# Two token tiles at once in the query and key norms of both attentions of a two-layer trunk

## The chip, the cores and the metric

The kernel runs on one core of a Trainium2 chip. The metric is the time of one execution on the device in microseconds (us); lower is better. Five engines work side by side, each through its own list of instructions in order: TensorE (PE, matrix products and transposes), VectorE (DVE), ScalarE (ACT), GpSimd (POOL) and SyncE (SP, which issues the DMAs here). They wait for one another through semaphores.

## The reference, cut to what matters

```python
def rmsnorm(x, g):
    y = x * rsqrt(mean(x * x, axis=-1) + 1e-6)
    return y * g

def attn_inputs(h, w_qkv, g_q, g_k, n_kv):
    y = h @ w_qkv                                   # 1024 -> q | k | v
    q = rmsnorm(per_head(y[..., :D_MODEL]), g_q)    # heads of 64
    k = rmsnorm(per_head(y[..., D_MODEL:...]), g_k)
    ...

for i in range(2):                                  # 1024 latent tokens, 256 context tokens
    h = modulate(rmsnorm(x, g_attn[i]), sh1, sc1)
    q, k, v = attn_inputs(h, ...)
    if i == 0: o = neighbourhood_attention(q, k, v, k_c, v_c, rpb)     # 16 heads
    else:                                           # 16 query heads, 4 key/value heads
        q, k = apply_rope(q, cos, sin), apply_rope(k, cos, sin)
        o = sliding_window_attention(q, k, v, k_c, v_c, sink)
    x = x + gt1 * (o @ w_out)
    x = x + gt2 * conv_ffn(modulate(rmsnorm(x, g_ffn[i]), sh2, sc2), ...)
```

## The kernel before

Tokens are cut into tiles of 128: eight latent ones (0 to 7) and two of context (8, 9). All is fp32; large products are made of three passes (high by high, low by high, high by low halves), which is why every weight and activation has a `hi` and a `lo` part.

The first attention goes through eight pairs of heads, and for each through the ten tiles in the order 8, 9, 0 to 7 (`plan_na_qkv`). Per tile: 24 products into a PSUM bank (`mm`), one ACT copy of all 384 columns (q, k, v) to SBUF (`qraw`), then the norm of four heads of 64 (`plan_rstd`): ACT squares (`qsq`), DVE sums per head (`qv`), DVE scales and adds epsilon (one instruction on 128x4), POOL raises to the power -0.5 (`qy`), DVE makes a Newton step (three instructions on 128x4, with `qt`), and DVE multiplies (`qn`). Two tiles' `qn` lie side by side, so that transposes, splits and later steps are already done by pairs of tiles. Around it, `plan_na_su` makes scores (`s`), bias, exponentials, scaling (`S`), transposes (`pt`) and the product with v (`pv`).

The second attention goes through four groups of heads (four query heads and one key head each), per group through tiles 0 to 7 (`plan_sw_qkv`), here tile by tile to the end: five heads normed, then the rotary products `qa` (by the cosine, on DVE or POOL, two instructions) and `qb` (by the sine, on POOL, four instructions), their sum on POOL (two instructions), three transposes on PE. `plan_sw_su` makes scores and the rest. Its softmax has a sink column, which POOL copies (`S<-small`).

The order of the work isn't that of the text. Each attention is planned by a list scheduler (`Sched`, L61): every operation gives its engine or engines, a cost, a key, what it reads and writes, and which buffers of a ring it takes and gives back; the planner walks through its own estimate of time, starts on each engine the operation with the lowest key that is ready and finds its buffers, and the order so found is then written out for every engine. A changed cost or a changed ring moves instructions on all five engines. At the end of each attention the output projection (`o0`, `o1`, `o2` parts) is planned in with the last scores. Weight halves of the next slab (`wlo<-slab`) are made on DVE or POOL.

Of the kernel before, what the change touches and what calls it, by code (L numbers as in the profile page):

```python
# [17 lines left out]
P = 128  # L18
# [205 lines left out]
def trunk_kernel(ctx, tc, xtok, xseq, cc, crow, wmod, wmodt, bmod, gnorm, na_wqkv, na_gqk, na_bias, na_wo,  # L224
# [111 lines left out]
    WG0, WG1 = 4, 5  # L336
    CONV_STEP = 1024
# [115 lines left out]
    def plan_qkv_mm(sc, key, psa, h, tt, slabs, s, J, c0=0, hkey=None):  # L453
# [3 lines left out]
        for kt in range(KT):  # L457
            def mm(e, kt=kt):
# [3 lines left out]
                for i, (a, w) in enumerate(((hh, wh), (hl, wh), (hh, wl))):  # L462
# [5 lines left out]
                  acq=[("mm", J["id"] + ("acc",), 1)] if kt == 0 else (), rel=[("w", i)] if kt % 2 else ())  # L468

    def plan_rstd(sc, key, J, c0, nh, wk, nsq):  # L470

        I = J["id"]

        def sq(e):
            J["sq"] = wk.tile([P, nsq], F32, tag="qsq", name="qsq", bufs=PTB["qsq"])
            act.activation(J["sq"][:, :nh * DH], J["raw"][:, c0:c0 + nh * DH], AF.Square)
        sc.op("act", t_act(nh * DH), sq, reads=[I + ("raw",)], writes=[I + ("sq",)], key=key, acq=[("qsq", I + ("sq",), 1)])

        def red(e):
            v = J["ms"] = tiny.tile([P, 5], F32, tag="qv", name="qv", bufs=4)  # L480
            dve.tensor_reduce(out=v[:, :nh], in_=J["sq"][:, :nh * DH].rearrange("p (h d) -> p h d", d=DH), axis=AX.X,
                              op=ALU.add)
        sc.op("dve", t_dve(nh * DH), red, reads=[I + ("sq",)], writes=[I + ("ms",)], key=key, rel=[I + ("sq",)])

        def mean(e):
            v = J["ms"][:, :nh]
            dve.tensor_scalar(out=v, in0=v, scalar1=1.0 / DH, scalar2=EPS, op0=ALU.mult, op1=ALU.add)
        sc.op("dve", t_dve(0), mean, reads=[I + ("ms",)], writes=[I + ("ms",)], key=key)

        def pw(e):  # L490
            J["y"] = tiny.tile([P, 5], F32, tag="qy", name="qy", bufs=4)
            J["t"] = tiny.tile([P, 5], F32, tag="qt", name="qt", bufs=4)
            pool.tensor_tensor(out=J["y"][:, :nh], in0=J["ms"][:, :nh], in1=mhalf[:, :nh], op=ALU.pow)
        sc.op("pool", 0.42 + nh * 0.165, pw, reads=[I + ("ms",)], writes=[I + ("y",)], key=key)
        ny = lambda: (J["y"][:, :nh], J["t"][:, :nh], J["ms"][:, :nh])

# [10 lines left out]
        for i in range(3):  # L507
            sc.op("dve", t_dve(0), newton(i), reads=[I + ("ms",)], writes=[I + ("y",)], key=key)

# [2156 lines left out]
```

## Time and profile before

| | us |
|---|---|
| three timed runs | 2758.87, 2759.04, 2761.37 (median 2759.04) |
| span of the profiled execution | 2755.5 |
| around the span (median less span; the profiled execution has no time of its own beside the three) | 3.5 |
| PE busy in the span | 2701.9 (98%) |
| DVE busy | 2247.1 (82%) |
| ACT busy | 1684.9 (61%) |
| POOL busy | 340.2 (12%) |

The span has four long stretches: the first attention (about 70 to 650 us), the first feed-forward block with the output projection ahead of it (to about 1610), the second attention (to about 2010) and the second feed-forward block. A table by stretch gives for each engine the busy time and the number of instructions, and the mean TensorE clock that was granted (1.00 is 2.4 GHz, 0.50 is 1.2 GHz). Groups of instructions are rows by operation and shape with busy time, mean duration of one in ns, and the idle time ahead of them with what ended it.

### The profile page before, as it was taken

What the parts mean: (1) busy time and instruction counts of PE and PEld (TensorE: products, weight loads), DVE (VectorE), ACT (ScalarE), POOL (GpSimd) and SP (SyncE); (2) the same over time, 40 slices, a digit from 0 to 9 for tenths busy, and PEclk for the clock granted to TensorE, in tenths of its full rate; (3) what the DMA queues carried; (4) which work ended last, traced back from release to release, by engine and by line L of the source; (5) the groups of instructions that cost most, each with busy time, mean ns of one, the idle gap of its engine ahead of it and who ended that gap; (6) DMA issues with size and microseconds to landing.
All of it is one profiled execution on the core that took longest, in us unless ns stands there. A gap on an engine that the chain in (4) does not pass through costs nothing.

```text
span 2755.5 us, 42708 instructions
## 1 busy us (share of the span) xinstructions
PE 2701.9 (98%) x15300; PEld 2282.4 (83%) x15300; DVE 2247.1 (82%) x4938; ACT 1684.9 (61%) x3000; POOL 340.2 (12%) x520
## 2 busy tenths in 40 slices
PE   7999999998999999999999999999999999999999
PEld 5999999987799988887888877777778788888887
DVE  5988888887778688787887889898877988888757
ACT  6777777776456555555564556666754666656443
POOL 1211111112000000000001007455410000000000
PEclk9999999999999999999999999999999999999999
DMA  7343343335656643334376562143243232334655
GB/s 263 98 127 117 117 135 119 111 96 165 216 170 184 184 142 104 129 118 135 119 249 198 188 201 68 43 129 102 78 152 113 88 115 100 112 107 146 234 175 186
DMA packets 147884, 387.89 MB, mean 141 GB/s; under 512 B 21332, under 2 KB 32084, under 8 KB 147288
## 3 DMA queue, kind: packets, MB, share of 16 engines
q1 hardware_dynamic: 147672, 385.17, 43.2%
q8 instruction: 120, 1.97, 0.3%
q14 instruction: 92, 0.75, 0.1%
HBM read 318.12 MB, written 66.99 MB: 140 GB/s over the span
## 4 chain that ended last, share of the span: by engine, by line
PE 76%; DVE 7%; DMA 2%; issue 2%; POOL 1%; ACT 1%; SPq 0%; DVEq 0%; ACTq 0%; POOLq 0%
PE ua L51 17%; PE uc L51 13%; PE dn L51 12%; PE mm L51 11%; PE pt L51 6%; PE oacc L51 4%; PE ud L51 4%; PE s L51 4%; PE dnc L51 2%; PE pv L51 2%; DVE S L51 1%; DVE wlo L51 1%; DMA woraw<-in_na_wo_dram 1%; DVE xn L51 1%; PE ug L51 0%
## 5 line engine op out<-in xcount | busy, mean ns | idle before, releaser
L51 ACT ACTIVATE whi<-wraw 128x512 fp32r<-128x512 f32 (+1 forms) x264 | 212.3, 804 | 153.6 <-PE uc L51 57.8
L51 DVE TENSOR_TENSOR wlo<-wraw,whi 128x512 fp32r<-128x512 f32 (+1 forms) x264 | 240.6, 912 | 47.7 <-ACT whi L51 47.3
L51 ACT ACTIVATE S<-S,m 128x640 f32<-128x640 f32 (+3 forms) x288 | 220.8, 768 | 63.2 <-DVE m L51 44.9
L51 PE MATMUL dn<-ghi,whi 128*128 128x512 f32 x616 | 240.0, 390 | 0.1
L51 PE MATMUL dn<-glo,whi 128*128 128x512 f32 x616 | 239.9, 389 | 0.2 <-DVE glo L51 0.2
L51 PE MATMUL dn<-ghi,wlo 128*128 128x512 f32 x616 | 239.8, 389 | 0.0
L51 ACT ACTIVATE whi<-s 128x1024 fp32r<-128x1024 f32 (+1 forms) x118 | 110.9, 941 | 182.1 <-PE uc L51 107.7
L51 POOL TENSOR_TENSOR qy<-qv,mhalf 128x4 f32<-128x4 f32 (+1 forms) x114 | 135.3, 1188 | 597.3 <-DVE qv L51 572.1
L51 PE MATMUL pt<-idr,S 128*128 128x128 f32 x1288 | 193.8, 277 | 11.9 <-DVE S L51 4.2
L51 PEld LDWEIGHTS pt<-idr,S 128*128 128x128 f32 x1288 | 151.5, 141 | 45.8 <-issue 12.0
L51 ACT ACTIVATE ghi<-graw 128x512 fp32r<-128x512 f32 x154 | 95.7, 628 | 144.5 <-PE dn L51 85.9
L51 PE MATMUL mm<-whi,h0hi 128*128 128x384 f32 x512 | 180.1, 352 | 0.0
L51 ACT ACTIVATE pt<-pt 128x512 f32<-128x512 f32 (+2 forms) x259 | 133.4, 535 | 64.6 <-PE pt L51 62.7
L51 PE MATMUL mm<-wlo,h0hi 128*128 128x384 f32 x512 | 172.1, 336 | 0.0
L51 DVE TENSOR_TENSOR glo<-graw,ghi 128x512 fp32r<-128x512 f32 x154 | 105.6, 695 | 78.1 <-ACT ghi L51 48.4
L51 DVE TENSOR_TENSOR wlo<-s,whi 128x1024 fp32r<-128x1024 f32 (+1 forms) x118 | 126.9, 1077 | 21.2 <-ACT whi L51 20.8
L51 PEld LDWEIGHTS dn<-ghi,whi 128*128 128x128 f32 x616 | 115.7, 188 | 24.6 <-issue 0.5
L51 PEld LDWEIGHTS dn<-glo,whi 128*128 128x128 f32 x616 | 115.7, 188 | 24.2 <-DVE glo L51 0.5
L51 PE MATMUL ua<-t12hi,whi 128*128 128x512 f32 x344 | 134.8, 392 | 0.9 <-ACT c L51 0.9
L51 PEld LDWEIGHTS dn<-ghi,wlo 128*128 128x128 f32 x616 | 115.6, 188 | 24.0
L51 PE MATMUL ua<-t12lo,whi 128*128 128x512 f32 x344 | 134.0, 390 | 0.0
L51 PE MATMUL ua<-t12hi,wlo 128*128 128x512 f32 x344 | 133.9, 389 | 0.0
(372 smaller groups left out, 8305.2 us busy)
## 6 DMA issues: line engine op xcount, KB each, us to landing
wraw<-in_w_up_dram SPq DMA_DIRECT2D x133, 512.0 KB, 3.8
wmt<-in_wmodt_dram SPq DMA_DIRECT2D x96, 512.0 KB, 4.0
wraw<-in_w_down_dram SPq DMA_DIRECT2D x44, 512.0 KB, 3.7
graw<-g_dram SPq DMA_DIRECT2D x44, 512.0 KB, 4.8
wraw<-in_w_down_dram SPq DMA_DIRECT2D x88, 256.0 KB, 3.0
graw<-g_dram SPq DMA_DIRECT2D x66, 256.0 KB, 2.8
wm<-in_wmod_dram SPq DMA_DIRECT2D x32, 512.0 KB, 6.7
slab<-in_na_wqkv_dram SPq DMA_DIRECT2D x32, 384.0 KB, 3.2
```

The costliest lines, as they stand in the source:

```text
L51: r = f(*a, **k)
```

## The change

Where the planner has seen the first tile of a pair it now only evacuates it; the norm is made for both tiles at the second one. In both attentions:

- the evacuation copies q and k alone (256 or 320 columns) into one half of a buffer of two tiles; v is copied from PSUM by an instruction of its own, and the PSUM bank is given back when both are done;
- one square, one sum per head, one power, one Newton step and one product with the norm for both tiles (8 heads in the first attention, 10 in the second);
- the division by 64 sits in the square's scale, and epsilon is added on POOL ahead of the power; the DVE instruction for both is gone. The Newton step has the same three instructions in another order of factors.

In the second attention also: the normed values go back into the buffer they came from, the squares lie in the buffer of the rotary product (`qa`, two buffers), and `qa`, `qb` and their sum are made for two tiles per instruction (the same number of instructions for two tiles as before for one). `qb` has one buffer. The context tiles of the second attention stay single, with the shorter norm. Counts of the instructions that the change touches (all others are as many, a few of them on another engine):

| | before | after |
|---|---|---|
| norm on DVE, first attention | 6 x 80 tiles | 5 x 40 pairs |
| norm on DVE, second attention | 6 x 32 tiles | 5 x 16 pairs |
| powers on POOL | 80, 32 | 40, 16 (each with an added 128x8 or 128x10 instruction) |
| `qa` on DVE / on POOL | 17 / 15 tiles | 13 / 3 pairs |
| `qb` and sum on POOL | 6 x 32 | 6 x 16 |
| PE | 14174 | 14174 |

```diff
-            act.activation(J["sq"][:, :nh * DH], J["raw"][:, c0:c0 + nh * DH], AF.Square)
+            act.activation(J["sq"][:, :n], src(), AF.Square, scale=DH ** -0.5)
...
-        def mean(e):
-            v = J["ms"][:, :nh]
-            dve.tensor_scalar(out=v, in0=v, scalar1=1.0 / DH, scalar2=EPS, op0=ALU.mult, op1=ALU.add)
-        sc.op("dve", t_dve(0), mean, reads=[I + ("ms",)], writes=[I + ("ms",)], key=key)
...
+            pool.tensor_scalar(out=v, in0=v, scalar1=EPS, scalar2=None, op0=ALU.add)
+            pool.tensor_tensor(out=J["y"][:, :nh], in0=v, in1=mhalf[:, :nh], op=ALU.pow)
+        sc.op("pool", 0.55 + nh * 0.165, pw, reads=[], writes=[I + ("ms",), I + ("y",)], key=key)
...
-    SBUFS, PTB = 5, dict(pt5=6, pt2=4, qsq=2)
+    SBUFS, PTB = 5, dict(pt5=6, pt2=4, qsq=1)
...
-    QA = (("dve", "pool"), (0.85, 1.1))
-    QB = ("pool", 1.55)
+    QA = (("dve", "pool"), (1.25, 1.9))
+    QB = ("pool", 2.1)
...
     def plan_na_qkv(n):
...
-            act.activation(J["raw"], J["acc"][:, :384], AF.Copy)
+            act.activation(f["raw", pr][:, tt % 2, :], J["acc"][:, :256], AF.Copy)
...
-            copy(e, f["v"][tt], pair(J["raw"][:, 256:384]))
+            copy(e, f["v"][tt], pair(J["acc"][:, 256:384]))
...
         if tt % 2 == 0:
             return
+        both = [two + ("raw", 0), two + ("raw", 1)]
+        plan_rstd(sc, key, J, 8, wk, 512, lambda: f["raw", pr].rearrange("p a b -> p (a b)"), both)
...
-    sc = Sched(dict(CAPS, pt5=6, pt2=3, qsq=1, q=10, S=SBUFS, s=4, qraw=3, qa=3, qn=3), near=3.0)
+    sc = Sched(dict(CAPS, pt5=6, pt2=3, qsq=1, q=10, S=SBUFS, s=4, qraw=3, qa=2, qb=1), near=3.0)
...
+            act.activation(B["raw"][:, tt % 2].rearrange("p h d -> p (h d)"), J["acc"][:, :320], AF.Copy)
...
+        plan_rstd(sc, key, B, 10, wk, 640, lambda: B["raw"].rearrange("p t h d -> p (t h d)"), both,
+                  (a_tile, [("qa", two + ("a",), 2)]))
...
+            r = B["raw"].rearrange("p t h d -> p (t h) d")
+            ENG[e].tensor_tensor(out=r, in0=r, in1=B["y"].unsqueeze(2).to_broadcast([P, 10, DH]), op=ALU.mult)
...
+                ENG[e].tensor_tensor(out=B["a"][:, :, s], in0=B["raw"][:, :, s], in1=tab(rc, k, m, slice(0, DH)), op=ALU.mult)
...
+            ENG[e].tensor_tensor(out=a[:, :, 5:6], in0=a[:, :, 4:5], in1=b[:, :, 4:5], op=ALU.add)
+            ENG[e].tensor_tensor(out=a[:, :, :5], in0=a[:, :, :5], in1=b, op=ALU.add)
+        sc.op("pool", t_pool(640) + t_pool(128), qs, reads=[K("b")], writes=[K("a")], key=key, rel=[K("b")])
+        for t in (tt - 1, tt):
+            plan_sw_tr(g, t, key, B, K)
```

Where it stands, at three places.

VectorE where the first attention's last products have ended and its last scores wait for buffers. Before (`S,m` and `m` are the evacuation of scores with its running minimum, named ISA where it adds the bias; the numbers are those of the scores' tiles):

```order
L51 TENSOR_REDUCE qv<-qsq 128x4
L51 CAST kll<-kll 64x256
L51 TENSOR_SCALAR qv<-qv 128x4
L51 TENSOR_SCALAR S,m_8462<-s 128x256
L51 COPY pt_8475<-pt 128x512
L51 COPY pt_8480<-pt 128x128
L51 ISA S,m_8462<-s,bias,m_8462 128x256
L51 ISA m_8462 128x1
L51 TENSOR_TENSOR qt<-qy 128x4
L51 TENSOR_SCALAR S,m_8495<-s 128x256
L51 SCALAR_TENSOR_TENSOR qt<-qt,qv 128x4
L51 ISA S,m_8495<-s,bias,m_8495 128x384
```

After:

```order
L51 TENSOR_TENSOR wlo<-woraw,whi 128x1024
L51 COPY v<-mm 128x128
L51 TENSOR_SCALAR S,m_8017<-s 128x256
L51 TENSOR_SCALAR S,m_8020<-s 128x256
L51 ISA S,m_8017<-s,bias,m_8017 128x384
L51 ISA m_8017 128x1
L51 ISA S,m_8020<-s,bias,m_8020 128x384
L51 ISA m_8020 128x1
L51 TENSOR_SCALAR S,m_8054<-s 128x256
L51 TENSOR_REDUCE qv<-qsq 128x8
```

The Newton step that stood between two evacuations stands behind them now; a weight half and a copy of v stand ahead.

GpSimd inside the second attention, from one power to the next. Before:

```order
L51 TENSOR_TENSOR qy<-qv,mhalf 128x5
L51 COPY S<-small 128x1
L51 TENSOR_TENSOR qa<-qn,rc 128x256
L51 TENSOR_TENSOR qa<-qn,rc 128x64
L51 COPY S<-small 128x1
L51 TENSOR_TENSOR qb<-qn,rs 128x4x32 x2
L51 TENSOR_TENSOR qb<-qn,rs 128x32 x2
L51 TENSOR_TENSOR qa<-qa,qb 128x64
L51 TENSOR_TENSOR qa<-qa,qb 128x320
```

After:

```order
L51 TENSOR_SCALAR qv<-qv 128x10
L51 TENSOR_TENSOR qy<-qv,mhalf 128x10
L51 COPY S<-small 128x1 x4
L51 TENSOR_TENSOR qb<-qraw,rs 128x2x4x32 x2
L51 TENSOR_TENSOR qb<-qraw,rs 128x2x32 x2
L51 TENSOR_TENSOR qa<-qa,qb 128x2x64
L51 TENSOR_TENSOR qa<-qa,qb 128x2x320
```

One such row of work serves two tiles, in wider instructions; most `qa` products have gone to VectorE.

TensorE at the last transposes of the second attention, among the output projection (`mm<-o0`). Before:

```order
L51 MATMUL pt<-idr,S 128x128 x10
L51 MATMUL s<-kkc_17655,q 128x256 x2
L51 MATMUL s<-kkl_17654,q 128x384 x2
L51 MATMUL pt<-idr,qa 128x128 x3
L51 MATMUL mm<-o0hi_22604,whi 128x512
```

After:

```order
L51 MATMUL pt<-idr,S 128x128 x2
L51 MATMUL mm<-o0hi_21664,whi 128x512
L51 MATMUL mm<-o0lo_21666,whi 128x512
L51 MATMUL mm<-o0hi_21664,wlo 128x512
L51 MATMUL pt<-idr,qa 128x128 x6
```

The transposes of two tiles stand together, with products of the projection ahead of them.

## Rows read from the trace of the kernel before

**Rows 1.** Busy time by stretch: bounds, length, each engine's busy us (instructions), clock, DMA

```profile
core 0: us, PE busy (x) PEld busy (x) DVE busy (x) ACT busy (x) POOL busy (x), PEclk, DMA share, GB/s
70.00:620.00 550.00, 546.68 (x3746) 502.65 (x3744) 479.11 (x1694) 408.35 (x964) 86.50 (x77) 1.00 0.37 115
620.00:650.00 30.00, 24.07 (x167) 19.78 (x166) 27.15 (x86) 23.84 (x52) 11.05 (x8) 0.89 0.49 153
...
1640.00:1980.00 340.00, 335.87 (x2296) 262.48 (x2296) 307.95 (x1021) 230.61 (x514) 187.61 (x362) 1.00 0.25 77
1980.00:2010.00 30.00, 26.40 (x175) 17.95 (x172) 28.12 (x85) 23.81 (x51) 13.88 (x30) 1.00 0.40 139
```

**Rows 2.** TensorE's waits from 620 to 650: who, for whom, total, times, longest

```profile
PE pt L51 <- DVE S L51: 1.5, 1, 1.5
PE s L51 <- DVE S L51: 1.4, 1, 1.4
```

**Rows 3.** Busy time by stretch, the seven microseconds behind those waits

```profile
623.00:630.00 7.00, 5.50 (x23) 4.38 (x25) 5.98 (x26) 5.72 (x12) 1.01 (x1) 0.53 0.75 235
```

**Rows 4.** GpSimd in order of time, 619 to 623: start, duration, what

```profile
619.45 2.36 POOL L51 TENSOR_TENSOR wlo<-woraw,whi 128x1024 fp32r<-128x1024 f32 x1
```

**Rows 5.** VectorE in order of time, the same stretch

```profile
619.98 1.86 DVE L51 TENSOR_TENSOR qt<-qy 128x4 f32<-128x4 f32 x1
```

**Rows 6.** TensorE's waits from 1640 to 1980

```profile
PE pt L51 <- DVE S L51: 2.0, 3, 1.3
PE pt L51 <- POOL qa L51: 1.0, 1, 1.0
```

**Rows 7.** GpSimd in order of time, 1786 to 1794

```profile
1789.74 3.74 POOL L51 TENSOR_TENSOR wlo<-slab,whi 128x768 fp32r<-128x768 f32 x2
```

**Rows 8.** VectorE in order of time, the same stretch

```profile
1791.66 2.17 DVE L51 TENSOR_SCALAR S<-S,sm 128x640 f32<-128x640 f32 x1
```

**Rows 9.** Groups by shape, 70 to 630: count, busy us, mean ns, idle before

```profile
L51 POOL TENSOR_TENSOR qy<-qv,mhalf 128x4 f32<-128x4 f32 x76 | 85.2, 1121 | 472.6 <-DVE qv L51 447.9 <-DVE sm L51 23.3 <-DVE qy L51 1.4
...
L51 DVE TENSOR_TENSOR qn<-qraw,qy 128x256 f32<-128x256 f32 x76 | 31.9, 420 | 0.3
...
L51 DVE TENSOR_REDUCE qv<-qsq 128x4 f32<-128x256 f32 x76 | 31.1, 410 | 1.7 <-ACT qsq L51 1.2
...
L51 DVE TENSOR_SCALAR qv<-qv 128x4 f32<-128x4 f32 x76 | 12.2, 161 | 0.2
```

**Rows 10.** Newton steps alone (VectorE instructions on `qt`), both attentions

```profile
70.00:630.00 560.00, 37.54 (x228) 0.99 0.37 116
1615.00:2015.00 400.00, 23.10 (x102) 1.00 0.30 96
```

**Rows 11.** Groups by shape, 1615 to 2015

```profile
L51 POOL TENSOR_TENSOR qy<-qv,mhalf 128x5 f32<-128x5 f32 x32 | 43.6, 1366 | 60.9 <-DVE qv L51 60.3
...
L51 POOL TENSOR_TENSOR qb<-qn,rs 128x128 f32<-128x128 f32 x64 | 31.7, 515 | 30.2 <-DVE qn L51 15.6 <-DVE sm L51 13.4 <-issue 1.2
L51 POOL TENSOR_TENSOR qa<-qa,qb 128x320 f32<-128x320 f32 x32 | 29.9, 935 | 2.5
L51 POOL COPY S<-small 128x1 f32<-128x1 f32 x122 | 29.9, 269 | 1.6 <-ACT S L51 1.6
...
L51 POOL TENSOR_TENSOR qb<-qn,rs 128x32 f32<-128x32 f32 x64 | 17.8, 298 | 0.0
L51 DVE TENSOR_TENSOR qn<-qraw,qy 128x320 f32<-128x320 f32 x32 | 16.1, 503 | 0.2
...
L51 DVE TENSOR_REDUCE qv<-qsq 128x5 f32<-128x320 f32 x32 | 15.3, 478 | 1.1 <-ACT qsq L51 1.0
...
L51 POOL TENSOR_TENSOR qa<-qa,qb 128x64 f32<-128x64 f32 x32 | 10.5, 329 | 0.5
...
L51 DVE TENSOR_SCALAR qv<-qv 128x5 f32<-128x5 f32 x32 | 8.2, 258 | 0.1
...
L51 DVE TENSOR_TENSOR wlo<-woraw,whi 128x1024 fp32r<-128x1024 f32 x4 | 4.9, 1219 | 0.4 <-ACT whi L51 0.4
```

## What was predicted

> **What bounds the kernel now.** I read the busy table first: TensorE is busy in 2701.9 of 2755.5 us (98%), and VectorE, whose work the change cuts, in 82%. The change leaves TensorE's 14174 instructions alone, so the time can fall only by what TensorE waits, or loses to a lower clock, in the two stretches that the change touches. The table by stretch gives that [rows 1]: length less PE's busy time is 3.3 us in the body of the first attention (550 - 546.68), 5.9 in its tail from 620 to 650, 4.1 in the body of the second (340 - 335.87) and 3.6 in its tail from 1980 to 2010. That is 16.9 us. One more loss hides in busy time: in the seven microseconds from 623 the granted clock is 0.53, about the lower of the two levels (1.2 GHz), right after TensorE stood still [rows 3]; 5.50 us of matmuls ran there, of which about 5.50 x (1 - 0.53) = 2.6 us would be gone at the full clock. So **19.5 us, 0.7%, is all that this change can reach**, whatever it saves elsewhere.
>
> Then I asked who ends those waits. From 620 to 650 the two largest, 1.5 and 1.4 us, are transposes and scores waiting for VectorE's evacuation of `S` [rows 2]. GpSimd makes a weight half at 619.45 (2.36 us) [rows 4], and the first Newton instruction, started beside it at 619.98, takes 1.86 us [rows 5], against a mean of 37.54 / 228 = 0.165 us [rows 10]: the tiny instruction ends only when GpSimd is done, and the evacuations queue behind it. In the second attention's body the listed waits are on VectorE's `S` (2.0 us in three) and on GpSimd's `qa` (1.0 in one) [rows 6], and the same sight stands at 1790: a weight half on GpSimd [rows 7], beside it the scaling of `S`, ahead of the transposes, takes 2.17 us [rows 8].
>
> **The change part by part.**
>
> *Norm, first attention.* Per pair before, on VectorE: two sums at 410 ns, two means at 161, six Newton instructions at 165, two products at 420 [rows 9, 10]: 820 + 322 + 990 + 840 = 2972 ns. After: the sum over twice the columns. How much of 410 is per column the trace tells by the second attention's 478 at 64 columns more [rows 11]: 68 per 64, so 410 + 4 x 68 = 682. The product likewise: 503 - 420 = 83 per 64, so 420 + 4 x 83 = 752. Three Newton instructions, 495; no mean. Sum 1929 ns, **1.05 us less per pair, 42 us over 40 pairs**. VectorE falls from 87% to about 79% of the body. It is not what bounds there, so nearly all of it is off the path: the body has 3.3 us of waits in 550. I give it -1.0, with 0 and -3.3 as ends.
>
> *Norm, second attention.* Per pair before 2 x (478 + 258 + 503) [rows 11] + 6 x 226 (23.10 / 102) [rows 10] = 3834 ns. After: 478 + 5 x 68 = 818, 503 + 5 x 83 = 918, 3 x 226 = 678: 2414. **1.4 us less per pair, 23 us over 16**, from 307.95 of 340 busy (91%) to about 85%. `qa` moves towards VectorE, from 17 tiles to 13 pairs: nine tiles more of 320 columns at 83 / 64 = 1.3 ns a column, 3.7 us, less eight instructions' fixed part of about 90 ns (420 - 4 x 83), 0.7: 3 us back.
>
> *GpSimd, second attention.* The power takes 1121 ns at 4 columns and 1366 at 5 [rows 9, 11], so 1366 + 5 x 245 = 2591 at 10, against 2 x 1366 = 2732; the added epsilon is bounded by the nearest small instruction there, 269 ns (`S<-small`). No gain. `qb`: 2 x 515 + 2 x 298 = 1626 per tile, 3252 a pair; with twice the columns 3 x 32 columns cost 217, so 128 columns more 289: 804, and 32 more 72: 370; 2 x 804 + 2 x 370 = 2348. The sum: 935 + 329 = 1264 per tile, 2528 a pair; its columns at (935 - 329) / 256 = 2.37 ns give 1692 + 480 = 2172. So 0.9 + 0.4 = **1.3 us less per pair on GpSimd**. It is 55% busy there (187.61 of 340): what counts of it is the chain, not the share.
>
> *The chain to TensorE, second attention.* From a tile's sum of squares to its transposes before: 478 + 258 + 678 + 1366 + 503 + 1626 + 1264 = 6.2 us. After, for two tiles: 818 + 269 + 678 + 2591 + 918 + 2348 + 2172 = **9.8 us**, 3.6 longer, and the first tile of a pair waits for its partner as well. What covers it is TensorE's work between a pair's last product and its transposes. In the written order the tightest place has 51 TensorE instructions after (49 before), the next ones 54, 73, 76 and 76; 335.87 / 2296 = 0.146 us each by busy time, somewhat more for products of 320 columns. So the cover is about 7.5 to 9 us at the two tightest pairs and 11 or more at the rest, against 9.8 us and the copy and the square ahead of it. I expect up to 2 us of new waiting at the tightest pairs, none at the others, and put **+1.0** (ends 0 and +4).
>
> *The tails.* At 620 the Newton step no longer stands between the score evacuations: they come first now, behind a weight half and a copy of v. The 1.86 us instruction [rows 5] isn't in that row any more, but that half, which GpSimd made in 2.36 us [rows 4], now stands on VectorE, at 1.22 us as four others do [rows 11]. The 2.9 us of waits [rows 2] and the 2.6 us of clock behind them hang together, since the clock fell after the standstill. I take **-4.0** of these 5.5; ends -5.5 and +1, where the half on VectorE delays the evacuations as much as the Newton step did. The second body: VectorE's lighter load and fewer small instructions that meet a GpSimd weight half (four per tile, now three per pair) take half of its 4.1: **-2.0** (ends -4.1, 0). Its tail has 3.6, where TensorE also waits for the last output parts that the change leaves alone: **-1.0** (ends -3, +1).
>
> *The rest.* The square on ScalarE covers two tiles in one instruction; the evacuation is 128 or 64 columns narrower, and the copy of v reads PSUM itself. ScalarE is 61% busy, so I put nothing there; uncovered, v's copy holding the product bank longer (0.4 us a tile at most, by the 410 ns of a 256-column sum [rows 9]) would cost that where the banks run out, which the waits of before don't list. The context tiles are too few to count.
>
> Sum: -1.0 - 4.0 - 2.0 - 1.0 + 1.0 = -7.0. The profiled span of 2755.5 becomes 2748.5; with the 3.5 us around it **2752.0**. Its own range, from the ends that can come together, is 2746 to 2757.
>
> A rule of the Trainium skill speaks against the change. What the rows show first: a VectorE instruction that touches SBUF alone, started beside a wide GpSimd one, lasts until that ends [rows 4, 5, 7, 8]. The skill ("SBUF — State Buffer", section "Who interferes with whom") says that VectorE and GpSimd share ports under a lock held for a whole instruction; it takes a two-input VectorE instruction or a fast mode to contend. By that, each wider GpSimd instruction holds VectorE longer. The trace agrees: the Newton product has two such inputs, the scaling can use a fast mode. By that rule alone the time would be that of the fourth case below.
>
> **The rivals.**
>
> *Nothing moves* (2759). The waits that VectorE's load seems to cause are only where the order was tight; the new order has as many, elsewhere. For it: PE waits only 3.3 us in 550 at a VectorE share of 87%, so less load need not mean less waiting. Against it: the named culprit at 620 is an instruction that the order moves. Price: none of the four gains, and the +1.0 unseen among them; give or take 3.
>
> *All of it goes* (2741). The waits and the lost clock go whole, 19.5 us, less some 1.5 us of the second tail's 3.6 that stay with the output parts: 2759 - 18. For it: VectorE gets 62 us of air. Against: in the tails the last scores follow one another through VectorE (27.15 of 30 us busy, and 28.12) [rows 1] whatever becomes of the norms.
>
> *Pairs come late* (slower, 2767). The longer chain isn't covered: each of the second attention's 16 pairs keeps TensorE waiting for its six transposes by 1 us (the wait on `qa` of before, 1.0 us in one place [rows 6], at every pair), +16, and the gains of 8 above stay. It decides where the cover is shorter than the chain: 9.8 us plus copy, square and queueing, from some 67 instructions of 0.146 us on. For it: one buffer of `qb`, two of `qa`, so pairs hardly overlap; GpSimd also makes weight halves of 3.74 us [rows 7] in between. Against it: only two places are below 67, the next is at 73.
>
> *The lock* (2758). A VectorE instruction caught by GpSimd's power is held for up to 2.6 us instead of 1.4, by its product `qb` and sum for 0.3 to 0.8 us more, and the evacuations behind it with it. If each of the three waits on `S` [rows 6] grows by the 1.2 us of the power, the second body loses 3 x 1.2 = 3.7 where I have -2.0, and the sum is -1.3. It decides where more than two such meetings reach TensorE. Against it: VectorE has half as many small instructions to be caught.
>
> **How the numbers follow.** Forecast 0.48; nothing moves 0.16; all goes 0.14; pairs late 0.16; the lock 0.06. A difference under 0.2% (5.5 us) is about what a measurement can't tell from none, so faster means under 2753.5, slower over 2764.6. Of the forecast's own range 2746 to 2757 I count 0.34 as faster and 0.14 as same. Faster: 0.34 + 0.14 = 0.48. Same: 0.14 + 0.16 + 0.06 = 0.36. Slower: 0.16. The range runs from 2739 (the large gain with 2 us to spare) to 2767 (the late pairs' middle): it leaves out half of that case and a little of the large gain, some 0.12.
>
> **What would show it.** Right: VectorE's busy time falls by about 60 us; from 620 to 650 PE busy comes to 26 or more of 30 at a clock near 1.00; the waits in the second attention stay below 4 us. Wrong: waits of transposes on `qa` in most of the 16 pairs (the pairs come late), or evacuations of `S` that last as long as a GpSimd instruction beside them (the lock), or TensorE's waits at their 17 us though VectorE has its air (nothing moves). A clock below 1.00 anywhere new would break the sum as well: it prices the clock at one place only.

## The result and the profile after

The changed kernel takes **2767.02 us** (median of 7 runs, 2763.11 to 2768.02) against 2758.87 before: a ratio of 1.0029, 95% interval 1.0019 to 1.0038. It is 8 us slower. The forecast was 2752.0, range 2739.0 to 2767.0; the median lies just outside, on the slow side.

The profiled execution has a span of 2766.0 us, 10.5 more than before. (Every execution here that has both a time and a span shows about 1.8 us around the span. So the profiled execution before took about 2757.3 us, less than the median, and 1.7 of the 3.5 us that the table of before puts around the span are scatter; the spans lie further apart than the medians by that.) Three matmuls that both kernels have mark its parts: the first product of the statistics after the first attention (`mp`), the one ahead of the second attention (`pt<-invd,sums`), and `mp` after the second attention. TensorE in order of time (start, duration, what, idle time before and its releaser); first the kernel before:

```profile
701.34 0.60 PE L51 MATMUL mp<-invd,nsum 128*128 128x1 f32 x4 [3.04 <-DVE nsum L51]
...
1627.94 1.05 PE L51 MATMUL pt<-invd,sums 128*128 128x1 f32 x8 [1.84 <-DVE sums L51]
...
2074.65 0.95 PE L51 MATMUL mp<-invd,nsum 128*128 128x1 f32 x8
```

and the changed kernel:

```profile
703.99 0.61 PE L51 MATMUL mp<-invd,nsum 128*128 128x1 f32 x4 [2.41 <-DVE nsum L51]
...
1629.77 1.08 PE L51 MATMUL pt<-invd,sums 128*128 128x1 f32 x8 [1.86 <-DVE sums L51]
...
2086.00 0.94 PE L51 MATMUL mp<-invd,nsum 128*128 128x1 f32 x8
```

So the first attention takes 2.7 us more (703.99 against 701.34) and the second 9.5 (456.2 against 446.7); the feed-forward parts differ by under 1 us each. The table by stretch of the changed kernel (columns as in [rows 1]), with the second attention's body also cut at 1740:

```profile
70.00:620.00 550.00, 544.94 (x3733) 500.28 (x3732) 463.46 (x1416) 394.06 (x939) 75.66 (x74) 1.00 0.38 115
620.00:650.00 30.00, 25.26 (x166) 20.98 (x164) 27.13 (x79) 23.35 (x51) 5.96 (x4) 0.89 0.36 113
...
1640.00:1740.00 100.00, 94.15 (x597) 78.11 (x599) 85.64 (x226) 58.20 (x128) 53.84 (x76) 0.97 0.25 77
1740.00:1980.00 240.00, 239.05 (x1663) 182.76 (x1660) 213.38 (x665) 163.18 (x368) 109.67 (x174) 1.00 0.25 79
...
1980.00:2010.00 30.00, 23.60 (x154) 16.95 (x153) 27.73 (x69) 21.04 (x44) 15.08 (x20) 0.94 0.39 132
```

The same cut before:

```profile
1640.00:1740.00 100.00, 99.42 (x658) 79.57 (x657) 94.49 (x298) 65.55 (x145) 63.38 (x117) 1.00 0.22 67
1740.00:1980.00 240.00, 236.45 (x1641) 182.91 (x1641) 213.46 (x724) 165.06 (x371) 124.23 (x246) 1.00 0.27 82
```

The middle of the second attention gained: TensorE idles for 0.95 us there in place of 3.55. Its first hundred microseconds lost: 5.85 in place of 0.58, at a granted clock of 0.97. Its tail lost too: 6.4 in place of 3.6, at 0.94 (1.00 before). The waits of TensorE from 1635 to 2020 (waiting tile, engine and tile waited for, total, times, longest), after:

```profile
PE pt L51 <- DVE S L51: 8.0, 3, 5.6
PE pt L51 <- ACT osb L51: 2.0, 1, 2.0
PE pt L51 <- DVE pt L51: 1.2, 3, 0.5
...
PE pt L51 <- POOL qa L51: 0.7, 2, 0.4
```

One wait of 5.6 us stands out, and almost none is for `qa`, the pairs' own result: 0.7 us in two. VectorE in order of time behind that wait, about the last pair:

```profile
2002.05 0.82 DVE L51 TENSOR_TENSOR qraw<-qraw,qy 128x640 f32<-128x640 f32 x1
2002.78 0.95 DVE L51 TENSOR_TENSOR o0lo<-osb,o0hi 128x256 fp32r<-128x256 f32 x1
2003.65 1.94 DVE L51 TENSOR_TENSOR qa<-qraw,rc 128x512 f32<-128x512 f32 x2
...
2005.98 1.64 DVE L51 TENSOR_SCALAR S<-S,sm 128x640 f32<-128x640 f32 x1
```

and GpSimd beside it:

```profile
2003.41 2.64 POOL L51 TENSOR_TENSOR qb<-qraw,rs 128x256 f32<-128x256 f32 x4
2006.01 1.26 POOL L51 TENSOR_TENSOR o0lo<-oraw,o0hi 128x512 fp32r<-128x512 f32 x1
```

The scaling of `S` that TensorE needs stands behind the norm product, an output half and two wide `qa` products, 3.5 us in all, and is then held beside a GpSimd half: 1.64 us where a mean one takes 0.60. TensorE stands still to 2007.76; its granted clock is 0.50 from 2008 to 2012, and 1.00 again from 2013 on.

The wait for `osb` is the largest of the first hundred microseconds. TensorE, ScalarE and GpSimd there:

```profile
1720.21 0.66 PE L51 MATMUL pt<-idr,S 128*128 128x128 f32 x4 [1.97 <-ACT osb L51]
```

```profile
1718.86 0.83 ACT L51 ACTIVATE S<-S,m 128x641 f32<-128x641 f32 x1 [2.86 <-POOL S L51]
```

```profile
1708.45 2.68 POOL L51 TENSOR_TENSOR qa<-qraw,rc 128x512 f32<-128x512 f32 x2 [9.83 <-PE s L51]
...
1711.32 3.96 POOL L51 TENSOR_TENSOR qb<-qraw,rs 128x256 f32<-128x256 f32 x4
1715.36 2.34 POOL L51 TENSOR_TENSOR qa<-qa,qb 128x128 f32<-128x128 f32 x2
1717.64 1.30 POOL L51 COPY S<-small 128x1 f32<-128x1 f32 x2
```

The copy of `osb` that TensorE waits for stands on ScalarE behind an exponential of `S`. That waits 2.86 us for a sink copy, which stands on GpSimd behind a pair's rotary products and their sum. The planner counts these at 1.9 + 2.1 + 1.9 = 5.9 us; they run from 1708.45 to 1717.70, 9.2 us. So a pair is late for TensorE here, but not through its own transposes.

At the end of the first attention it is the same sight as [rows 4, 5], ten microseconds later: TensorE waits 3.93 us from 631 for a copy on VectorE that stands behind the last pair's Newton step and product, and the first Newton instruction is held to the end of a weight half on GpSimd:

```profile
634.93 1.12 PE L51 MATMUL pt<-idr,qn 128*128 128x128 f32 x4 [3.93 <-DVE pt L51]
```

```profile
630.15 2.31 DVE L51 TENSOR_TENSOR qt<-qv,qy 128x8 f32<-128x8 f32 x1 [0.18 <-POOL qy L51]
```

```profile
630.08 2.35 POOL L51 TENSOR_TENSOR wlo<-woraw,whi 128x1024 fp32r<-128x1024 f32 x1
```

The Trainium skill ("SBUF — State Buffer", section "Who interferes with whom") names such a hold between a VectorE instruction with two SBUF inputs and a GpSimd instruction that reads SBUF. The last two rows agree: the Newton product takes 2.31 us beside a half of 2.35, where such an instruction takes about 0.165 on average. Why an instruction was put beside that half, or ahead of that scaling, the rows don't tell. That is a question to the order, and the experiments are about it.

Most prices of single instructions came out near the forecast; the power and the epsilon did not. Groups by shape of the changed kernel, answering [rows 9] and [rows 11] (count, busy us, mean ns, idle before); first attention, then second:

```profile
L51 POOL TENSOR_TENSOR qy<-qv,mhalf 128x8 f32<-128x8 f32 x38 | 66.1, 1739 | 3.2
L51 DVE TENSOR_REDUCE qv<-qsq 128x8 f32<-128x512 f32 x38 | 25.9, 681 | 0.6 <-ACT qsq L51 0.4
L51 DVE TENSOR_TENSOR qn<-qraw,qy 128x512 f32<-128x512 f32 x37 | 25.5, 690 | 0.5
L51 POOL TENSOR_SCALAR qv<-qv 128x8 f32<-128x8 f32 x38 | 11.5, 302 | 482.7 <-DVE qv L51 340.2 <-DVE sm L51 142.4
```

```profile
L51 POOL TENSOR_TENSOR qy<-qv,mhalf 128x10 f32<-128x10 f32 x16 | 32.2, 2015 | 1.3
L51 POOL TENSOR_TENSOR qb<-qraw,rs 128x256 f32<-128x256 f32 x32 | 29.9, 955 | 39.2 <-DVE qraw L51 23.6 <-DVE sm L51 15.6
...
L51 POOL TENSOR_TENSOR qa<-qa,qb 128x640 f32<-128x640 f32 x16 | 25.0, 1560 | 1.3
...
L51 DVE TENSOR_TENSOR qraw<-qraw,qy 128x640 f32<-128x640 f32 x16 | 13.1, 820 | 0.1
L51 DVE TENSOR_REDUCE qv<-qa 128x10 f32<-128x640 f32 x16 | 13.0, 810 | 0.0
L51 POOL TENSOR_TENSOR qb<-qraw,rs 128x64 f32<-128x64 f32 x32 | 12.4, 408 | 0.0
...
L51 POOL TENSOR_TENSOR qa<-qa,qb 128x128 f32<-128x128 f32 x16 | 8.4, 528 | 0.7
...
L51 POOL TENSOR_SCALAR qv<-qv 128x10 f32<-128x10 f32 x16 | 6.5, 404 | 57.4 <-DVE qv L51 42.6 <-DVE sm L51 14.4
```

GpSimd's part of a pair's chain is thus 404 + 2015 + 2 x 955 + 2 x 408 + 1560 + 528 = 7.2 us.

### The profile page after: what moved, and what is told of

Read it like the earlier page. It is cut to its first block, busy times and chain, and to the rows that moved or that the text cites. A ratio compares the mean times of both kernels' runs of the same rounds, so it can differ in the third digit from the quotient of the medians.

```text
span 2766.0 us, 42172 instructions
## 1 busy us (share of the span) xinstructions
PE 2705.4 (98%) x15300; PEld 2285.1 (83%) x15300; DVE 2231.6 (81%) x4511; ACT 1668.4 (60%) x2971; POOL 302.8 (11%) x400
## 4 chain that ended last, share of the span: by engine, by line
PE 68%; DVE 5%; issue 1%; POOL 1%; DMA 1%; ACT 1%; SPq 0%; DVEq 0%; POOLq 0%; ACTq 0%
PE ua L51 17%; PE dn L51 13%; PE uc L51 13%; PE mm L51 5%; PE pt L51 5%; PE oacc L51 4%; PE ud L51 4%; PE s L51 2%; PE dnc L51 2%; DVE S L51 1%; DVE wlo L51 1%; DVE xn L51 1%; PE ug L51 0%; PE mod L51 0%; DMA slab<-in_sw_wqkv_dram 0%
## 5 line engine op out<-in xcount | busy, mean ns | idle before, releaser
L51 DVE CUSTOM_DVE_ANT_0 wmt<-wmt,crow,bmod_t 128x1024 f32<-128x1024 f32 x96 | 129.3, 1350 | 3.6 <-DMA wmt<-in_wmodt_dram 2.6
```

The source lines that it names most:

```text
L51: r = f(*a, **k)
```

## The experiments

All ratios are against runs of the kernel before on the same chip, with 95% intervals.

### One attention at a time

The pairs in the first attention alone, or in the second alone; the other keeps its old code, buffers and planner's costs.

> Pairs in the first attention only; the second attention as before, with its own planner costs and buffers. In the changed kernel the end of the first attention's projection comes 2.7 us later than before. If that is what the pairs cost there, this kernel takes 2759 + 3 = 2762 us. If the loss lies in the second attention alone and the 2.7 us are chance, 2759. If the pairs gain in the first attention once its tail is right, under 2756. The waits ahead of the transposes of qn (1.5 us in three between 70 and 622, 3.9 us at 635) should be there again, since the order up to that place is the same as in the changed kernel.

> Pairs in the second attention only; the first attention as before. In the changed kernel the second attention and its tail lose 8.7 us against before. If the two parts add up, this kernel takes 2759 + 8 = 2767 us or a little less, and TensorE stands still for 5 to 6 us at the end of the second attention while VectorE makes the norm product and qa of the last pair. If the loss there depended on when the first attention ends, it falls under 2763.

Measured: 2769.1 us (1.0038, 1.0025 to 1.0050) and 2771.2 us (1.0049, 1.0035 to 1.0062). Each alone is slower than both together; that can't be the pairs. The groups by shape showed where: the products `dn` of the feed-forward blocks, which the edit doesn't touch. first_only:

```profile
L51 PE MATMUL dn<-ghi,whi 128*128 128x512 f32 x616 | 242.4, 394 | 0.0
```

against 390 ns before; 1848 such matmuls at 4 ns are 7 us. With two versions of the norm these kernels held 240 bytes more of small tiles, so I let both versions share the old space:

> Pairs in the first attention only, as in first_only, but the small tiles of both norms share the space that they have before, so that no other buffer changes its address. Theory: in first_only and second_only the 1848 matmuls dn of the feed-forward blocks took 393 ns in place of 389 since their buffers lay 240 bytes further, which is 7 us of their 11 and 13. Then dn is back at 389 to 390 ns and this kernel takes 2762 us (the 2.7 us that the first attention loses in the changed kernel). If the addresses have nothing to do with it, 2769 as before.

> Pairs in the second attention only, with the small tiles in the space that they have before. Theory: dn at 389 to 390 ns, and 2759 + 8 = 2766 us. Together with first_fit this then adds up to what the changed kernel loses, most of it in the second attention. If addresses have nothing to do with it, 2771.

Measured: 2759.05 us (1.0008, 0.9999 to 1.0017) and 2764.25 us (1.0021, 1.0012 to 1.0030), with `dn` at 389 and 390 ns. Now the parts add up: 1.7 and 7 us. The loss lies mostly in the second attention; that of the first alone isn't clear of noise by its time.

These kernels also show how far one profile can be trusted. Up to the first mark, the five that have tiles in the first attention, under the same plan, lie between 699.5 and 702.5 us (kernel before, second_only, second_fit and, further down, before_shift and before_lead); the five with pairs, under the changed kernel's costs, between 704.0 and 706.1 (changed kernel, first_only, first_fit, sw_ends, after_lead). The second attention takes 446.5 to 450.6 us in four kernels with tiles under the plan of before and 454.9 to 456.2 in three with pairs under the changed kernel's. So both attentions lose, and differences of 2 to 4 us between two single profiles say little.

Whether the 240 bytes did it as a shift of addresses was tried on the kernel before, with `[P, 92]` in place of `[P, 32]` in an unused tile:

> The kernel before with an unused tile ahead of the other buffers made 240 bytes larger, nothing else, so that buffers behind it lie 240 bytes further. If addresses set the duration of the matmuls dn, as first_only against first_fit suggests, dn takes 393 to 394 ns in place of 390 and the time rises by 6 to 8 us to 2764 to 2766. If the small tiles' sharing did it, nothing changes: 2756 to 2760.

Measured: 2758.8 us (1.0007, 0.9998 to 1.0015), `dn` at 389 to 390 ns. A shift of that tile does nothing. What made `dn` slower in the first two kernels stays open; they are used no further.

### Held instructions: GpSimd's halves in the tails

```diff
-            sc.op(("pool", "dve"), (t_pool(n), t_dve(n)), lo, reads=reads + [("oh",) + name], writes=[("ol",) + name], key=key,
+            sc.op("dve", t_dve(n), lo, reads=reads + [("oh",) + name], writes=[("ol",) + name], key=key,
...
-            sc.op(*((("pool", "dve"), (2.28, 1.13)) if self.shared else ("dve", t_dve(1024))), lo, reads=[r, ("woh", i)],
+            sc.op("dve", 1.13, lo, reads=[r, ("woh", i)],
```

> The changed kernel, with all low halves of the output projection (weights, and the o parts) made on VectorE; GpSimd makes none in the two tails. Theory of collisions: VectorE's instructions are held in both tails by GpSimd's halves (2.31 us for a Newton instruction at 630, 1.64 us for a scaling of S at 2006), so the two standstills of 3.9 and 5.6 us shrink to under 2 each and the time falls to 2760 or below. Theory of bulk: the pair's wide products stand ahead of the scaling of S on VectorE whoever makes the halves; the standstill at the end of the second attention stays above 3 us, and with more work on VectorE the time stays at 2764 or rises.

> The kernel before with the same edit: all low halves of the output projection on VectorE. Theory of collisions: the waits of 1.5 and 1.4 us at 622 to 625 and the lower clock behind them go, time 2753 to 2757. Theory of bulk: VectorE, 27 to 28 us busy in each tail of 30, gets 5 to 8 us more to do there, and the time rises by 2 to 6 us.

Measured: 2762.3 us (1.0018, 1.0009 to 1.0027) and 2754.6 us (0.9989, 0.9980 to 0.9998). By the ratios each gains about 3 us (1.0029 to 1.0018, and 1 to 0.9989); for the changed kernel the two intervals overlap. GpSimd's halves in the tails cost something, but as much before as after: they aren't what the change lost. In the changed kernel a wait of 4.0 us is left up to 2002. Holds beside other GpSimd work, in the bodies, were not taken out: the changed kernel's second largest wait for `S`, 1.65 us up to 1687.86, is for a scaling of 1.84 us beside a weight half.

### Filling and draining; the width itself

sw_ends takes the first pair of the first group and the last pair of the last group tile by tile; all_single takes every pair so.

```diff
+    SW1 = ((0, 0), (3, 3))
...
-        if tt % 2 == 0:
-            return
+        if (g, pr) in SW1:
+            stage(g, pr, (tt % 2,), key, two, both, B)
+        elif tt % 2:
+            stage(g, pr, (0, 1), key, two, both, B)
```

> The changed kernel, but the first pair of the first group and the last pair of the last group of the second attention are normed and rotated tile by tile (narrower instructions, same buffers); the other 14 pairs stay. Theory of filling and draining: the loss of the second attention lies where nothing else is ready for TensorE, at its first pair (5.2 us more waiting and a lower clock from 1640 to 1740) and at its last (4 to 5 us after 1985); then this kernel gets most of it back and takes 2758 to 2762. Theory of late pairs: each of the 16 pairs costs some; two of them are 1 us, and the time stays at 2764 to 2767.

> The changed kernel with every pair of both attentions normed tile by tile: the shorter norm with epsilon on GpSimd, the copy of v from PSUM and the normed values in place stay, only the width of two tiles is undone. If the width is the cause of the whole loss, about the time before, 2756 to 2761. If the other parts of the change cost something, 2763 or more, and the waits lie elsewhere than at the ends of the attentions.

Measured: 2765.1 us (1.0026, 1.0015 to 1.0037) and 2767.1 us (1.0030, 1.0018 to 1.0041). Filling and draining aren't the cause: with single tiles at the ends the waits only changed places (2.04 us at 1685 for ScalarE's `S`, 1.53 at 1998 for VectorE's, and now 3.1 us in four for `qa`).

all_single is as slow as the changed kernel as a whole, but loses at other places. Its second attention takes 449.5 us, within the range of the kernels with tiles and 6.8 less than the changed kernel's 456.2; its first takes 709.0, longer than any other here. So the equal times don't show that the width costs nothing. all_single isn't the kernel before either: it has the smaller rings of the changed kernel and its added epsilon on GpSimd, and GpSimd's part of its chain is planned at 4.0 us and takes 4.8, with 6.2 us of waits for `qa` in six. What all these versions share is a new plan, made with costs that nobody had fitted to the new instructions; that is the next suspect.

### The order by itself

The scores of the second attention set back by one tile: `LEAD1` 9.1 in place of 7.5.

> The changed kernel, with the keys of the second attention's scores set back by one tile (9.1 in place of 7.5), since a pair is ready when its second tile is. Theory of filling: the 6.4 us of waits between 1640 and 1760 fall to under 3, since products of the next tiles come ahead of scores that aren't ready, 2761 to 2764; the tail gets longer by the work set back, at most 2 us. Theory of a tuned order: a few us to either side, waits at other places.

> The kernel before with the same set-back of one tile and nothing else. Theory of a tuned order: 2760 to 2766, that is 2 to 8 us lost by nothing but another order. Theory that order alone is worth little: 2756 to 2759.

Measured: 2766.3 us (1.0030, 1.0018 to 1.0041) and 2757.7 us (0.9999, 0.9990 to 1.0008). This other order costs the kernel before nothing and brings the changed one nothing: a move by itself need not spoil the order, and scores set back by one tile are not the cure.

### The planner's costs

The planner orders each engine by its own estimate. In the changed kernel it counts the sine products of a pair at 2.1 us, the power with epsilon at 0.55 + 10 x 0.165 = 2.2 and the sum at 1.9: 6.2 us where the trace has 7.2, 1 us or 14% short. Before it was (1.25 + 1.55 + 1.10) = 3.9 against 1.37 + 1.63 + 1.26 = 4.3, 8% short. The edit of after_costs sets the costs to the trace of the changed kernel (but for `qa` on VectorE, whose two instructions take 1.6 us a pair on average and get 1.45):

```diff
-    QA = (("dve", "pool"), (1.25, 1.9))
-    QB = ("pool", 2.1)
+    QA = (("dve", "pool"), (1.45, 2.15))
+    QB = ("pool", 2.75)
...
-        sc.op("pool", 0.55 + nh * 0.165, pw, reads=[], writes=[I + ("ms",), I + ("y",)], key=key)
+        sc.op("pool", 0.7 + nh * 0.17, pw, reads=[], writes=[I + ("ms",), I + ("y",)], key=key)
...
-        sc.op("pool", t_pool(640) + t_pool(128), qs, reads=[K("b")], writes=[K("a")], key=key, rel=[K("b")])
+        sc.op("pool", 2.1, qs, reads=[K("b")], writes=[K("a")], key=key, rel=[K("b")])
```

> The changed kernel, with the planner's costs set to the durations that its trace shows: the sine products of a pair 2.75 us in place of 2.1, the power with epsilon 2.06 (8 heads) and 2.4 (10) in place of 1.87 and 2.2, the sum 2.1 in place of 1.9, qa 1.45 and 2.15 in place of 1.25 and 1.9. Theory of the mis-planned chain: GpSimd's part of the chain is planned at 6.2 us and takes 7.2, so whatever needs it is ordered a little early; with the true costs the second attention gets 3 to 6 us back, 2761 to 2764. Theory of a tuned order: the constants of before fit its order by trial, any other order loses some; the time moves by a few us to either side, and the waits are at other places.

> The changed kernel with true costs and with all low halves of the output projection on VectorE (the edit that took the changed kernel from 2767 to 2762 and the kernel before from 2758 to 2755). If the two gains are of different places and add up, 2757 to 2760. If both only shuffle the order, 2761 to 2766.

Measured: **2750.8 us** (0.9972, 0.9963 to 0.9982), and 2752.4 us (0.9982, 0.9973 to 0.9991) with the halves on VectorE as well. Only the order differs, and on which of two engines a few operations run; 16 us are gone, and the kernel is faster than before. That is more than either theory expected, and half of it lies in the first attention, where none was expected (see below). With that order the halves on VectorE bring nothing any more. To tell truth from luck, the same costs were made too short once more, too long, and longer still, and the kernel before got true and long costs too:

> The changed kernel with its planner's costs made as much too short again: sine products 1.45 (they take 2.73), the sum 1.7 (2.1), the power 1.68 and 2.0 (2.04 and 2.4), qa 1.05 and 1.65. Theory of the mis-planned chain: TensorE's transposes are ordered still earlier than they can be ready; 2768 to 2780, with waits on GpSimd's qa or on what stands behind them. Theory of a tuned order or of chance: no direction, 2750 to 2770.

> The changed kernel with costs as much too long as they are too short in it: sine products 3.4 (2.73), the sum 2.3 (2.1), the power 2.25 and 2.6 (2.04 and 2.4), qa 1.65 and 2.4. Theory of the mis-planned chain: work is ordered late enough, so no new waits on the chain; the price is only what is put off at the two ends of the attention: 2750 to 2757. Theory of chance: no direction, 2750 to 2770.

> The changed kernel with costs still longer: sine products 4.05 (they take 2.73), sum 2.5 (2.1), power 2.6 and 2.95 (2.04 and 2.4), qa 1.85 and 2.65. So far the order is 2772 (short), 2767 (as written), 2751 (true), 2746 (long). If the chain is covered from true costs on, more brings nothing: 2744 to 2750. If work is put off too far, the ends of the attentions lose: 2752 to 2760.

> The kernel before with the planner's costs set to the durations of its own trace: the power 1.12 and 1.37 us in place of 1.08 and 1.25, the sine products 1.63 in place of 1.55, the sum 1.26 in place of 1.10, qa 0.88 and 1.28 in place of 0.85 and 1.10. Its chain on GpSimd was planned at 3.9 us and takes 4.3, a smaller error than the changed kernel's. Theory of the mis-planned chain: a gain of 0 to 3 us, 2755 to 2758, so that the pairs with true costs (2751) stay ahead of the tiles with true costs. Theory that the true costs were worth the 16 us by chance, as another order: anything from 2750 to 2765.

> The kernel before with costs on GpSimd's chain too long by about as large a share as in costs_long: power 1.30 and 1.57 us (they take 1.12 and 1.37), sine products 1.95 (1.63), sum 1.4 (1.26), qa 0.97 and 1.45. If generous costs are what makes costs_long fast (2746), with or without pairs, this kernel takes 2746 to 2751. If the pairs bring the gain and the costs only let it through, 2752 to 2757.

| second attention's sine products planned at | whole part on GpSimd planned at | kernel | us | ratio, interval |
|---|---|---|---|---|
| 1.45 (take 2.73) | 5.2 (takes 7.2 to 7.5) | costs_short | 2772.5 | 1.0052, 1.0039 to 1.0065 |
| 2.1 | 6.2 | changed kernel | 2767.0 | 1.0029, 1.0019 to 1.0038 |
| 2.75 | 7.2 | after_costs | 2750.8 | 0.9972, 0.9963 to 0.9982 |
| 3.4 | 8.3 | costs_long | **2746.1** | 0.9957, 0.9944 to 0.9970 |
| 4.05 | 9.5 | costs_longer | 2749.3 | 0.9971, 0.9962 to 0.9980 |
| tiles, 1.55 (take 1.63) | 3.9 (takes 4.3) | kernel before | 2758.9 | 1 |
| tiles, 1.63 | 4.3 | before_costs | 2754.3 | 0.9989, 0.9980 to 0.9998 |
| tiles, 1.95 | 4.9 | before_long | 2762.6 | 1.0015, 1.0006 to 1.0024 |

With pairs, short costs lose and true or long ones gain; between the three that gain the intervals overlap. For costs_short and costs_long the direction was forecast, and it came true. With tiles only the true costs gain: before_long is as much too long as costs_long (some 15%) and loses, outside both of its expectations; the cause is open. What short costs do is plain in costs_short. The first of its waits of TensorE from 1635 to 2020 is now the chain's own; the second is the standstill of 2002 again, a little later:

```profile
PE pt L51 <- POOL qa L51: 6.9, 8, 1.6
PE pt L51 <- ACT S L51: 4.8, 2, 4.5
```

and in after_costs, the same stretch:

```profile
PE pt L51 <- DVE S L51: 2.6, 3, 1.4
PE pt L51 <- ACT pt L51: 1.9, 3, 0.7
PE pt L51 <- ACT q L51: 1.8, 2, 1.5
PE pt L51 <- DVE pt L51: 1.0, 1, 1.0
PE pt L51 <- POOL qa L51: 0.5, 1, 0.5
```

In costs_long the wait on `qa` isn't listed. ScalarE's waits for sink copies on GpSimd, which held `osb` at 1718, go the same way. Changed kernel, then costs_long, same stretch:

```profile
ACT S L51 <- POOL S L51: 19.9, 13, 4.1
```

```profile
ACT S L51 <- POOL S L51: 8.2, 6, 2.3
```

The others, by rising cost: 20.7 us in costs_short, 13.2 in after_costs, 1.7 in costs_longer; 9.2 in the kernel before. From a pair's last evacuation of products to its first transposes TensorE runs at least 60 instructions in costs_short, 62 in the changed kernel, 83 in after_costs, 95 in costs_long and 84 in costs_longer (counted in the traces). The marks of after_costs:

```profile
694.74 0.54 PE L51 MATMUL mp<-invd,nsum 128*128 128x1 f32 x4
...
1620.04 1.53 PE L51 MATMUL pt<-invd,sums 128*128 128x1 f32 x8 [1.86 <-DVE sums L51]
...
2067.10 0.94 PE L51 MATMUL mp<-invd,nsum 128*128 128x1 f32 x8
```

Against the changed kernel the first attention is 9.3 us shorter and the second 9.2 (447.1); against the kernel before, 6.6 shorter and 0.4 longer. costs_long reads 694.3 and 445.9, costs_short 704.7 and 458.9. So what the pairs gain over the tiles, they gain in the first attention; the second only comes back to where it was. Long costs alone don't make a kernel fast: the kernel before gained 3.5 us by true costs and lost 4.6 by long ones. With each at the best costs tried, measured side by side, pairs take 2746.1 and tiles 2754.3.

A rival is chance: every order is a draw, and some draws are good. Against it, the four kernels with pairs in both attentions and costs of the trace or longer take 2746.1 to 2752.4 us, and the five with costs as first written or shorter 2762.3 to 2772.5, without overlap. For it speaks before_long alone, where an order moved by 8 us against before_costs for no known reason.

Two things aren't settled. The four costs were changed together, so which of them counts in the second attention wasn't told apart. And in the first attention only the power's cost differs (1.87, then 2.06 for eight heads, which take 2.04): 0.2 us a pair takes 9 us off, as a step and not as a slope (704.7 and 704.0 us with short costs, 694.7, 694.3 and 697.3 with true and longer ones). Some 6 us of that step are waits that are gone in after_costs: the 2.41 us ahead of `mp`, and 3.4 of the 4.55 us for which TensorE idles from 650 to 690. Why the order turned there wasn't tried.

## Why the prediction was wrong

*What bounds the kernel* was right in kind: only TensorE's waits and clock could move, and the loss is there. (The trace counts 15300 TensorE instructions in either kernel, not 14174; that they are as many holds.) The ceiling of 19.5 us was too low. It left out 3.04 us of waiting ahead of `mp` at 701, and the clock of 0.91 from 690 to 710; in after_costs TensorE is busy for all of these 20 us, at 1.00.

*The prices* were near where they had rows. First attention: sum 681 ns (682 forecast), product 690 (752), the three Newton instructions by their groups about 165 each. Second: sum 810 (818), product 820 (918), sine products 955 and 408 (804 and 370), the closing sum 2088 (2172). The power was the worst, 2015 ns against 2591, since two points of 4 and 5 columns gave too steep a slope; epsilon took 404 against 269.

*VectorE's relief* was mis-sized. In the body of the first attention its busy time fell by 15.6 us (479.11 to 463.46), not by 42; over both bodies by 25, not by about 60. The durations were right: summed over the trace, those of the norm fall by 41.6 us in the first body (110.6 to 69.0), and those of all else on VectorE hardly rise (468.2 to 471.1). But a sum of durations overstates what small instructions hold: they overlap. Behind the held instruction at 630 the rows of VectorE are

```profile
632.92 0.15 DVE L51 SCALAR_TENSOR_TENSOR qt<-qt,qy 128x8 f32<-128x8 f32 x1
633.00 0.15 DVE L51 RECIPROCAL sm<-sm 128x1 f32<-128x1 f32 x1
633.11 0.17 DVE L51 SCALAR_TENSOR_TENSOR qy<-qt,qy 128x8 f32<-128x8 f32 x1
```

Each starts 0.08 to 0.11 us after the one ahead, for a duration of 0.15 to 0.17.

*The chain to TensorE, +1.0*, is the step that failed. It priced a longer chain only by the pairs' own transposes, and took the new order for granted besides; the second attention, forecast at -2.0 - 1.0 + 1.0 = -2.0, measured +9.5. The chain's length was right: 9.6 us by the groups (0.81 + 0.40 + 2.02 + 0.70 + 0.82 + 2.73 + 2.09), 9.8 forecast. Its cover, counted in the written order, was nearly enough, as I had found: the transposes wait 0.7 us for `qa`. But the order is the planner's, made with 6.2 us for the part on GpSimd that I had just priced at 269 + 2591 + 2348 + 2172 = 7.4. I had both numbers, one of them in the diff, and didn't set them side by side. A cost that is short doesn't only make its own result late: all that the planner puts on an engine after it is timed by it. For sink copies behind wide sums the rows at 1718 show it, and ScalarE's waits of 19.9 us that fall as the costs rise. That scalings of `S` land behind wide products for the same reason fits the runs, since the wait at 2002 stays with costs_short and goes with after_costs, but the single cost behind it wasn't tried.

*The tails, -4.0 and -1.0*. From 620 to 650 TensorE idles 1.2 us less than before (4.74 against 5.93), at the same clock of 0.89, where 26 us of work and a clock near 1.00 were to show that the forecast was right; from 650 to 690 it idles 2.5 us more. The second tail lost 2.8 us where it was to gain 1.0. The instruction that caused the wait at 620 did go from its place, as the order said; it met another half at 630. I had followed one hold to its removal, and not asked where the next Newton step would fall.

*The second body, -2.0*, was right for its middle: 2.6 us less idle from 1740 to 1980. Its first hundred microseconds lost 5.3, which the forecast hadn't as a place of its own; the wait for `osb` is part of that.

*The rivals.* "Pairs come late" gave 2767, the measured time, for a reason that isn't this kernel's: waits on `qa` are 0.7 us in two, not 1 us in 16. In costs_short its mechanism is real (6.9 us in eight). "Nothing moves" had the mechanism that came nearest, as many waits elsewhere in the new order; it is more of them, and 2759 was too low. "The lock" was there in both kernels, and its part in the tails worth about 3 us to either; its part in the bodies wasn't measured. (The 3.74 us of [rows 7] are two halves in a row, as the x2 says.) The forecast of 2752 is near the 2750.8 that the change gives once its costs are true, but that is in part luck: by the profiles the first attention then gains 6.6 us where the sum had 5.0, some of it at places that the sum left out, and the second nothing where it had 2.0.

## What to carry to other kernels

When an edit changes how long an operation takes in a kernel whose order comes from a list scheduler, its costs are part of the edit: set every changed cost against a duration from rows, for a chain as a sum, before believing the order. Short costs on the long chain lost 8 to 15 us here in the kernel with pairs; costs too long by 15% gained there and lost with tiles, so too long is no safe side either. A fair comparison of two designs gives each its own true costs. Look for the price of a late chain also in what stands behind it on its engine, not only at its end. Don't sum durations of instructions of 0.15 us as if they stood end to end.

## What the runs showed of the hardware

- Small VectorE instructions overlap: 0.15 us of duration, 0.08 us from start to start.
- The products `dn` took 393 to 394 ns in two kernels (first_only, second_only) whose edits didn't touch them, and 389 to 390 in all others, 7 us in the whole. A plain shift of 240 bytes didn't bring it about; the cause is open.
- GpSimd's power costs 1121, 1366, 1739 and 2015 ns for 4, 5, 8 and 10 columns: about 150 ns a column from 4 to 10, though 245 from 4 to 5.
